# Splitting the first rotary query weights beside the retention stage's last gate tile, and the latents' first half in pieces of 256 columns

## The chip, the cores and the metric

The kernel runs on one core of a Trainium2 chip. A core has five engines with instruction queues of their own: PE (TensorE: matrix products, its weight loads shown as PEld), DVE (VectorE), ACT (ScalarE), POOL (GpSimd) and SP (SyncE, which here issues nearly all DMAs). Each works through its own queue in the order in which the program was built and waits there on semaphores. The metric is the device time of one execution in microseconds (us); lower is better.

## The reference, cut to what matters

One layer of a hybrid decoder: 1024 prompt tokens and 32 sample tokens, all in float32. Both pass through a retention branch and an attention branch over compressed latents; the branches are gated, merged and added to the input.

```python
# mixer_inputs: one projection of the normalised input gives all of these
z = rmsnorm(x, ln_w) @ w_in
rq, rk, rv, rg, cq, ckv, kr, mg, ga, gb = split(z)      # mg: attention's SiLU gate
q = (rmsnorm(cq, q_norm_w) @ w_uq).reshape(b, s, MLA_HEADS, MLA_QK)   # 8 heads of 128 + 64
q_nope, q_rope = q[..., :128], rope(q[..., 128:], pos)
ckv, kr = rmsnorm(ckv, kv_norm_w), rope(kr, pos)
# mla_prompt: latents (384 for queries, 256 for keys and values) of 1024 tokens
kv = (ckv @ w_ukv)                                       # k_nope, v per head
sc = (q_nope . k_nope + q_rope . kr) * scale             # causal softmax, then p @ v
# finish_layer
h_mla = (mla_o * silu(mg)) @ w_down_mla
```

## The kernel before

**Precision.** Each float32 operand is split in two parts: `hi`, a rounded copy made by ACT or POOL, and `lo`, the remainder, made by DVE (`lo_of`, line 199). A product is three matmuls (`mac`, lines 265, 266 and 267: hi by hi, the two mixed ones). In the profile's names a pair reads `wh`/`wl` (weights), `xh`/`xl` (normalised input), `lh`/`ll` (latents), `krA`/`krB` (rotary keys).

**Weights.** `stage` (lines 245, 246) loads a piece of weights into a staging tile `wr` with an SP DMA, makes `hi` and `lo`. There are two staging tiles, and two pairs of weight tiles `wh`, `wl`. Who makes `hi` is set by `hi_by[0]`: `act.copy` in the retention stage, `hi_pool` (POOL) from the start of prompt attention on.

**Stages around the change.** Retention runs head by head. Beside the last head's chunks and the sample tokens' state update (`sample_state`, lines 978 to 1057) stands a filler: the last three tiles of the gate `mg` (`gate_tiles`, tiles 5, 6 and 7). A tile has 8 x 128 weight rows against three thirds of 352 tokens, so 24 matmuls a third; ACT evacuates a third (`gev`, line 416) and SP stores it (line 417, `mg_95` is tile 5, `mg_96` tile 6, `mg_97` tile 7). The latents `lat` and rotary keys `krT` are loaded in the meantime from a scratch area in device memory to slots of the tags `qkA` and `qkB`.

Then the retention pools close, and prompt attention opens: its tiles take the memory of the retention stage, `krA` and the mask `above` that of the last head's output tiles `g`, the split latents `lh`, `ll` and the split rotary query weights `wqr` that of the normalised input. `rope_weights(0)` loads and splits three pieces (128 x 256) of `w_uq`; `split_latents` splits five latents of 1024 columns in halves of 512; `rope_queries` makes the first four heads' rotary query parts, eight tiles of 128 tokens with nine matmuls each, woven with head 0's queries, keys and values.

**What sets the order.** The code yields estimated costs and `woven` mixes streams by them, and then a scheduler sets the order in each engine's queue, so that an instruction may stand far from its place in the code. Only marked matmuls (`keep_in_program_order`, line 1041) are held.

Of the kernel before, what the change touches and what calls it, by code (L numbers as in the profile page):

```python
# [9 lines left out]
F32 = mybir.dt.float32  # L10
# [3 lines left out]
AF = mybir.ActivationFunctionType  # L14
# [5 lines left out]
P = 128  # L20
D = 1024
SEQ = 1024
# [11 lines left out]
HM = 8  # L34
NOPE = 128
ROPE = 64
# [7 lines left out]
C_RQ, C_RK, C_RV, C_RG, C_LAT, C_MG, C_GA, C_GB = 0, 1024, 2048, 4096, 6144, 6848, 7872, 8896  # L44
# [70 lines left out]
def woven(*streams):  # L115

    live = [[g, float(total), 0.0] for g, total in streams]
    while live:
        s = min(live, key=lambda e: e[2] / e[1])
        cost = next(s[0], None)  # L120
        if cost is None:
            live.remove(s)
            continue
        s[2] += cost
        yield cost
# [30 lines left out]
def run(g):  # L156
    for _ in g:
        pass
# [3 lines left out]
def decode_step(ctx: ExitStack, tc: tile.TileContext, A: dict, O: dict):  # L162
    nc = tc.nc
    pe, act, dve, pool, sp = nc.tensor, nc.scalar, nc.vector, nc.gpsimd, nc.sync

    const = ctx.enter_context(tc.tile_pool(name="const", bufs=1))
    wst = ctx.enter_context(tc.tile_pool(name="wst", bufs=2))
# [20 lines left out]
    def slots(pl, tag, bufs):  # L188

        return lambda name, shape=(P, NT), dt=F32R: pl.tile(list(shape), dt, tag=tag, name=name, bufs=bufs)  # L190

    def b32(ap):
        return ap.bitcast(F32)
# [4 lines left out]
    def lo_of(out, src, hi):  # L198
        dve.tensor_tensor(out=out, in0=src, in1=b32(hi), op=ALU.subtract)  # L199
# [4 lines left out]
    def C(name, i=0, w=None, rows=P):  # L204
        o, ww = at[name]
        w = ww if w is None else w
        return cst[:rows, o + i * w:o + (i + 1) * w]
# [10 lines left out]
    mgD = [dram.tile([P, NT], F32, tag=f"mg{f}", name=f"mg{f}") for f in range(8)]  # L218
# [7 lines left out]
    def small(pl, tag, w=1, bufs=4):  # L226
        return pl.tile([P, w], F32, tag=tag, name=tag, bufs=bufs)
# [9 lines left out]
    hi_by = [hi_pool]  # L237
# [11 lines left out]
    def wtiles():  # L249
        return tuple(wst.tile([P, 8, P], F32R, tag=t, name=t, bufs=2) for t in ("wh", "wl"))  # L250

    def load_w(src, nk):

        hi, lo = wtiles()
        src = src.rearrange("(k p) f -> p k f", p=P)
        for k in range(0, nk, 4):
            ks = slice(k, min(k + 4, nk))
            stage(src[:, ks], hi[:, ks], lo[:, ks])
        return hi, lo

    def mac(out, w, x, first, last):

        wh, wl = w
        xh, xl = x
        pe.matmul(out, wh, xh, start=first, stop=False)  # L265
        pe.matmul(out, wh, xl, start=False, stop=False)  # L266
        pe.matmul(out, wl, xh, start=False, stop=last)  # L267

    def gemm(w, xs, evac, nk, thirds_=range(3)):

        for j in thirds_:
            ps = mm()
            sl = slice(j * TH, (j + 1) * TH)
            for k in range(nk):
                mac(ps[:, :TH], (w[0][:, k, :], w[1][:, k, :]), (xs[k][0][:, sl], xs[k][1][:, sl]), k == 0, k == nk - 1)
                if k == nk - 1:
                    evac(j, ps[:, :TH], sl)
                yield 0.441
# [131 lines left out]
    def gate_tiles(col, dst, fs, func):  # L410
        for f in fs:
            w = load_w(w_in[:, col + f * P:col + (f + 1) * P], 8)

            def evac(j, ps, sl, f=f):
                t = wst.tile([P, TH], F32, tag="gev", name="gev", bufs=2)
                act.activation(t, ps, func)  # L416
                sp.dma_start(dst[f][:, sl], t)
            yield from gemm(w, xn, evac, 8)

    def chain(*gs):  # L420
        for g_ in gs:
            yield from g_
# [4 lines left out]
    def page_rows():  # L427
# [6 lines left out]
        row = small(p1, "row", NB * NPG // 16, 1)  # L434
        dve.tensor_reduce(out=row, in_=own, axis=AX.X, op=ALU.add)
        dve.tensor_scalar(idx, row, C("mod"), None, op0=ALU.add)
# [157 lines left out]
    def new_tokens(g):  # L594
# [20 lines left out]
        dve.tensor_tensor(out=pn, in0=sc[:H, :NR], in1=cst[:H, o:o + NR], op=ALU.add)  # L615
        dve.tensor_reduce(out=nm[:H], in_=pn, axis=AX.X, op=ALU.max, negate=True)
        act.activation(pn, pn, AF.Exp, bias=nm[:H], accum_out=l[:H])
# [150 lines left out]
    qkA, qkB = slots(qk8, "qkA", 4), slots(qk8, "qkB", 4)  # L768
# [16 lines left out]

    def head_qk(h, X):
        for name, col in (("q", C_RQ), ("k", C_RK)):
            dst = X[name] = [tok(f"{name}{m}", dt=F32) for m in range(2)]

# [23 lines left out]
            for m, evac in enumerate((first, second)):  # L813
                w = load_w(w_in[:, col + h * DK + m * P:col + h * DK + (m + 1) * P], 8)
                yield from gemm(w, xn, evac, 8)
            own = X[name + "S"] = p4.tile([P, 2, NR], F32, tag=name + "S", name=name + "S", bufs=2)
            for m in range(2):
                act.copy(own[:, m], dst[m][:, SEQ:])

    def head_w(h, X):  # L820

        parts = [[sl_("wv", (P, 2, DV)) for _ in range(4)] for sl_ in (qkA, qkB)]
        X["W"] = [tuple(part[k // 2][:, k % 2, :] for part in parts) for k in range(8)]
        for k in range(8):
            stage(w_in[k * P:(k + 1) * P, C_RV + h * DV:C_RV + (h + 1) * DV], *X["W"][k])
            yield 1.0
# [155 lines left out]
    def sample_state(h, X):  # L982
# [79 lines left out]
        else:  # L1062
            gate_out(h, on, NR, sl, g)
            yield 0.5

    def head_in(h, X):
        return woven((head_qk(h, X), 42.3), (head_w(h, X), 8.0))

    X = {}
    run(head_in(0, X))  # L1070
    for h in range(HR):
        chunks = prompt_chunks(h, X)
        for cost in chunks:
            if cost is None:
                break
        nxt = {}
        if h + 1 < HR:
            rest = (head_in(h + 1, nxt), 50.3)
        else:
            rest = (gate_tiles(C_MG, mgD, range(5, 8), AF.Silu), 31.8)  # L1080
            raws = [(qkB if i < 4 else qkA)("lat", (P, SEQ), F32) for i in range(5)]
            for i, raw in enumerate(raws):
                sp.dma_start(raw, latD[4 * i:4 * i + 4].rearrange("b i t -> (b i) t"))
            krT = qkA("krT", (P, SEQ), F32)
            for r in range(0, P, ROPE):
                sp.dma_start(krT[r:r + ROPE], latD[20:].rearrange("b i t -> (b i) t"))
        run(woven((chain(chunks, sample_state(h, X)), 27.9 if h + 1 < HR else 32.4), rest))
        X = nxt
    hi_by[0] = hi_pool
# [5 lines left out]
    ot = slots(mph.enter_context(tc.tile_pool(name="mla", bufs=1, side="right")), "ot", HM)  # L1095
# [19 lines left out]
        lo_of(lo, ps, hi)  # L1115

    lat = [tuple(latp.tile([P, SEQ], F32R, tag=f"l{s}{i}", name=f"l{s}{i}") for s in "hl") for i in range(5)]
    def split_latents(some):
        for u in range(2):
            us = slice(u * 512, (u + 1) * 512)  # L1120
            for i in some:
                hi, lo = (v[:, us] for v in lat[i])
                (hi_pool if i == 1 and u == 0 else act.copy)(hi, raws[i][:, us])
                lo_of(lo, raws[i][:, us], hi)
                yield 0.1

# [6 lines left out]
            split(krT[:, us], krA[:, us], krB[:, us])  # L1133
            yield 0.1

    HB = 4

    def rope_weights(h0):
        if h0:
            hi, lo = (v.rearrange("p (k x) d -> p k (x d)", k=4)[:, :3] for v in wtiles())  # L1140
        else:
            hi, lo = (ot("wqr", (P, 3, HB * ROPE)) for _ in range(2))
        for k in range(3):
            if k % 2 == 0:
                raws_ = wst.tile([P, 2, HB, ROPE], F32, tag="wr", name="wr", bufs=2)
            raw = raws_[:, k % 2]
            sp.dma_start(raw, A["w_uq"][0, k * P:(k + 1) * P, :].rearrange("p (h d) -> p h d", h=HM)[:, h0:h0 + HB, NOPE:])
            parts = [v[:, k].rearrange("p (h d) -> p h d", h=HB) for v in (hi, lo)]
            hi_by[0](parts[0], raw)
            lo_of(parts[1], raw, parts[0])  # L1150
        return hi, lo

    first_w = rope_weights(0)
    run(split_latents(range(3)))

    def rope_queries(h0, X):

        qrN = X["qrN"] = p5.tile([P, 8, HB * ROPE], F32, tag="qrN", name="qrN", bufs=1)
        hi, lo = rope_weights(h0) if h0 else first_w
        for t in range(8):  # L1160
            ps = mm() if h0 else ac()
            ts_ = slice(t * P, (t + 1) * P)
            for k in range(3):
                mac(ps[:, :256], (cqn[k][0][:, ts_], cqn[k][1][:, ts_]), (hi[:, k], lo[:, k]), k == 0, k == 2)
            rope_nat(qrN[:, t, :].rearrange("p (h d) -> p h d", h=HB), ps[:, :256].rearrange("p (h d) -> p h d", h=HB), t, P, p5, HB, "qro")
            yield 1.0
# [185 lines left out]
    for h in range(HM):  # L1352
        ahead = prep(h + 1) if h + 1 < HM else iter(())
        owed = 0.0
        if h + 1 == HM:
# [6 lines left out]
            first_w = load_w(A["w_down_mla"][0, :, :P], 8)  # L1362
# [128 lines left out]
    for f in range(8):  # L1491
# [3 lines left out]
        hi, lo = xr_("x1h"), xr_("x1l")  # L1495
# [10 lines left out]
        if f in (3, 4):  # L1506
            k = f - 3
# [73 lines left out]
    for j in range(3):  # L1581
        u = third(j, pT)
# [43 lines left out]
```

## Time and profile before

| | |
|---|---|
| median of 3 runs | 2147.01 us (2147.0 to 2148.47) |
| profiled execution | 2157.48 us, span 2155.6 us |
| mean granted TensorE clock | 0.996 |
| PE busy | 2112.4 us, 98% of the span |
| DVE, ACT, POOL busy | 58%, 34%, 15% |
| DMA | 307.84 MB, mean 143 GB/s |

The profile is of one execution, and its times are told from the span's start. The gate tiles' last part and the opening lie between about 1300 and 1380 us. A row of the timeline gives start, duration, engine, line and operation, result<-operands, count, and in brackets the idle time of the engine before it and what ended it. A row of a view by windows gives the stretch, its length, busy time (and instructions) of PE, PEld, DVE, ACT and POOL, then the granted clock (1.00 is full), the DMA engines' busy share and the transfer rate in GB/s. A row of waits gives who waited for whom, the total in us, how often and the longest.

### The profile page before, as it was taken

The numbers are of one execution on the slowest core, as the hardware profiler recorded it, in microseconds if no ns is written. First come the engines' busy times: TensorE is split into PE (matmuls) and PEld (weight loads), VectorE is DVE, ScalarE is ACT, GpSimd is POOL, SyncE is SP. The second block draws the span as 40 slices with busy tenths as digits, with TensorE's granted clock in tenths as the row PEclk, the third lists the DMA queues.
The fourth block names the chain that finished last, engine by engine and source line by source line (L and its number), as shares of the span: only waits on it lengthen the run. The fifth ranks groups of instructions, "written<-read, shape, count | busy, mean of one in ns | idle before, by whom it ended". The sixth has DMA issues, their size and how long they took to land. (4 is left out here: it accounts for less than half of the span.)

```text
span 2155.6 us, 38512 instructions
## 1 busy us (share of the span) xinstructions
PE 2112.4 (98%) x15192; PEld 1841.9 (85%) x15192; DVE 1260.7 (58%) x2846; ACT 724.1 (34%) x1528; POOL 326.7 (15%) x519
## 2 busy tenths in 40 slices
PE   8999999999999999999999999899999999999998
PEld 7898777777778897888888887788888999999998
DVE  5534555565655346667676774877777353444465
ACT  5412222433433222222222221454556341222243
POOL 2210111111100022222122220122221000000022
PEclk9999999999999999999999999999999999999999
DMA  7476656566565332553634628220112453324243
GB/s 209 123 223 225 238 185 231 200 245 222 186 239 176 112 85 65 162 158 103 217 72 126 198 74 265 69 53 12 38 57 81 143 178 100 95 84 126 79 143 118
DMA packets 325877, 307.84 MB, mean 143 GB/s; under 512 B 91648, under 2 KB 283264, under 8 KB 321600
## 3 DMA queue, kind: packets, MB, share of 16 engines
q1 hardware_dynamic: 316480, 221.50, 34.3%
q0 software_dynamic: 9216, 83.89, 10.3%
q8 instruction: 119, 1.95, 0.4%
q14 instruction: 62, 0.51, 0.1%
HBM read 236.96 MB, written 68.36 MB: 142 GB/s over the span
## 5 line engine op out<-in xcount | busy, mean ns | idle before, releaser
L265 PE MATMUL mm<-xh,wh 128*128 128x352 f32 x1344 | 456.6, 340 | 0.9 <-ACT gev L416 0.8
L267 PE MATMUL mm<-xh,wl 128*128 128x352 f32 x1344 | 435.2, 324 | 2.1 <-DVE wl L199 2.1
L266 PE MATMUL mm<-xl,wh 128*128 128x352 f32 x1344 | 436.1, 324 | 0.0
L265 PEld LDWEIGHTS mm<-xh,wh 128*128 128x128 f32 x1344 | 253.2, 188 | 91.5 <-issue 77.2
L266 PEld LDWEIGHTS mm<-xl,wh 128*128 128x128 f32 x1344 | 254.3, 189 | 3.2 <-issue 1.0
L267 PEld LDWEIGHTS mm<-xh,wl 128*128 128x128 f32 x1344 | 253.9, 189 | 3.3 <-DVE wl L199 2.6
L199 DVE TENSOR_TENSOR wl<-wr,wh 128x512 fp32r<-128x512 f32 (+2 forms) x251 | 172.9, 701 | 121.2 <-ACT wh L246 99.6
L246 ACT CAST wh<-wr 128x512 fp32r<-128x512 f32 x216 | 129.7, 618 | 291.9 <-PE mm L266 215.6
L651 DVE STREAM_TRANSPOSE kt<-craw 128x512 f32<-128x512 f32 x256 | 160.8, 681 | 108.3 <-PE sc L655 73.2
L416 ACT ACTIVATE gev<-mm 128x352 f32<-128x352 f32 x120 | 55.4, 463 | 231.6 <-PE mm L267 149.8
L265 PE MATMUL mm<-mh,wh 128*128 128x352 f32 x384 | 124.6, 325 | 1.4 <-ACT mh L1109 0.8
L266 PE MATMUL mm<-ml,wh 128*128 128x352 f32 x384 | 124.6, 325 | 0.8 <-DVE ml L199 0.6
L267 PE MATMUL mm<-gh,wl 128*128 128x352 f32 x384 | 124.3, 324 | 0.0
L267 PE MATMUL mm<-mh,wl 128*128 128x352 f32 x384 | 124.3, 324 | 0.0
L265 PE MATMUL mm<-gh,wh 128*128 128x352 f32 x384 | 124.2, 324 | 0.0
L266 PE MATMUL mm<-gl,wh 128*128 128x352 f32 x384 | 124.2, 323 | 0.0
L265 PE MATMUL mm<-wv,xh 128*128 128x512 f32 x256 | 103.7, 405 | 0.0
L266 PE MATMUL mm<-wv,xh 128*128 128x512 f32 x256 | 100.9, 394 | 0.0
L267 PE MATMUL mm<-wv,xl 128*128 128x512 f32 x256 | 100.8, 394 | 0.0
L655 PE MATMUL sc<-kt,q 32*32 32x512 f32 x2560 | 92.9, 600 | 0.0
L854 ACT ACTIVATE on<-ac,gb,gs 128x512 f32<-128x512 f32 (+1 forms) x36 | 28.0, 777 | 179.6 <-DVE gb L852 179.6
L1556 POOL TENSOR_TENSOR xr<-x1h,x1l 128x352 f32<-128x352 f32 x24 | 27.1, 1152 | 389.4 <-DVE pT L199 311.3
(383 smaller groups left out, 4537.6 us busy)
## 6 DMA issues: line engine op xcount, KB each, us to landing
wr<-in_w_in_dram SPq DMA_DIRECT2D x144, 256.0 KB, 2.8
st<-in_state_ret_dram SPq DMA_DIRECT2D x32, 512.0 KB, 4.5
out_ret_sample_dram<-st SPq DMA_DIRECT2D x32, 512.0 KB, 3.2
wr<-in_w_ple_gate_dram SPq DMA_DIRECT2D x48, 256.0 KB, 2.9
gt<-gev SPq DMA_DIRECT2D x48, 176.0 KB, 1.9
gl<-go SPq DMA_DIRECT2D x16, 528.0 KB, 5.2
gate<-ga SPq DMA_DIRECT2D x16, 528.0 KB, 3.6
g<-gt SPq DMA_DIRECT2D x32, 256.0 KB, 3.4
```

The lines of the kernel that those rows point to most:

```text
L199: dve.tensor_tensor(out=out, in0=src, in1=b32(hi), op=ALU.subtract)
L246: hi_by[0](hi, raw)
L265: pe.matmul(out, wh, xh, start=first, stop=False)
L266: pe.matmul(out, wh, xl, start=False, stop=False)
L267: pe.matmul(out, wl, xh, start=False, stop=last)
L416: act.activation(t, ps, func)
L651: dve.transpose(kt[:, 2 * i + s].rearrange("p (n r) -> p n r", r=32), src)
L655: pe.matmul(sc[32 * v:32 * v + 32, q, :], Q["q4"][qs_, j + v // 2, 2 * (g % 2) + v % 2, :], kt[qs_, v, :], start=n == 0, stop=n == NJ // 2 ...
L854: act.activation(on[:n], po, AF.Identity, bias=nb[:n], scale=s[:n])
L1556: pool.tensor_tensor(out=xr, in0=b32(x1[f][0][:, sl]), in1=b32(x1[f][1][:, sl]), op=ALU.add)
```

## The change

`rope_weights` moves ahead in the code and is called for the first four heads between gate tiles 6 and 7, as a part of the filler (`early`). Its `wqr` tiles take slots of the tag `qkB` instead of prompt attention's `ot`; to make room, three of the five latents move to `qkA` and two stay in `qkB`. At that point `hi_by[0]` is `act.copy`, so ACT makes the `hi` parts of `wqr`, not POOL. `split_latents` takes its pieces as an argument, and the three query latents' first half is split in two pieces of 256 columns; the second half stays whole.

```diff
+    def rope_weights(h0):
+        if h0:
+            hi, lo = (... for v in wtiles())
+        else:
+            hi, lo = (qkB("wqr", (P, 3, HB * ROPE)) for _ in range(2))
+        for k in range(3):
+            if k % 2 == 0:
+                raws_ = wst.tile([P, 2, HB, ROPE], F32, tag="wr", name="wr", bufs=2)
+            raw = raws_[:, k % 2]
+            sp.dma_start(raw, A["w_uq"]...[:, h0:h0 + HB, NOPE:])
...
+            hi_by[0](parts[0], raw)
+            lo_of(parts[1], raw, parts[0])
+        return hi, lo
...
-            rest = (gate_tiles(C_MG, mgD, range(5, 8), AF.Silu), 31.8)
-            raws = [(qkB if i < 4 else qkA)("lat", (P, SEQ), F32) for i in range(5)]
+            raws = [(qkA if i < 3 else qkB)("lat", (P, SEQ), F32) for i in range(5)]
...
+            def early():
+                first_w.extend(rope_weights(0))
+                yield 0.0
+            rest = (chain(gate_tiles(C_MG, mgD, range(5, 7), AF.Silu), early(), gate_tiles(C_MG, mgD, range(7, 8), AF.Silu)), 31.8)
...
-    def split_latents(some):
-        for u in range(2):
-            us = slice(u * 512, (u + 1) * 512)
+    def split_latents(some, parts=((0, 512), (512, SEQ))):
+        for a, b in parts:
+            us = slice(a, b)
             for i in some:
                 hi, lo = (v[:, us] for v in lat[i])
-                (hi_pool if i == 1 and u == 0 else act.copy)(hi, raws[i][:, us])
+                (hi_pool if i == 1 and a < 512 else act.copy)(hi, raws[i][:, us])
                 lo_of(lo, raws[i][:, us], hi)
...
-            hi, lo = (ot("wqr", (P, 3, HB * ROPE)) for _ in range(2))
...
-    first_w = rope_weights(0)
-    run(split_latents(range(3)))
+    run(split_latents(range(3), ((0, 256), (256, 512), (512, SEQ))))
```

The instructions' order as built shows where the scheduler puts the moved steps. SP's queue from the first store of gate tile 6 to tile 7's, before:

```order
L417 DMA mg_96<-gev 128x352
L978 DMA st<-in_state_ret_dram 128x2x512 x2
L1049 DMA out_ret_sample_dram<-st 128x2x512 x2
L417 DMA mg_96<-gev 128x352
L978 DMA st<-in_state_ret_dram 128x2x512 x2
L1049 DMA out_ret_sample_dram<-st 128x2x512 x2
L417 DMA mg_96<-gev 128x352
L1147 DMA wr<-in_w_uq_dram 128x4x64
L1049 DMA out_ret_sample_dram<-st 128x2x512 x2
L417 DMA mg_97<-gev 128x352
L1147 DMA wr<-in_w_uq_dram 128x4x64 x2
```

The same stretch of SP's queue with the change:

```order
L417 DMA mg_96<-gev 128x352
L978 DMA st<-in_state_ret_dram 128x2x512 x2
L1049 DMA out_ret_sample_dram<-st 128x2x512 x2
L417 DMA mg_96<-gev 128x352
L978 DMA st<-in_state_ret_dram 128x2x512 x2
L1049 DMA out_ret_sample_dram<-st 128x2x512 x2
L417 DMA mg_96<-gev 128x352
L245 DMA wr<-in_w_in_dram 128x4x128 x2
L245 DMA wr<-in_w_uq_dram 128x3x128
L245 DMA wr<-in_w_ukv_dram 128x2x128 x2
L1049 DMA out_ret_sample_dram<-st 128x2x512 x2
```

The two loads of tile 7's weights (`in_w_in_dram`) stand here now, behind tile 6's last store. Before, they stood where the last head's first key blocks (`kD`) are written, and the query weights' loads stand at that place now, as the difference of SP's queue there shows:

```order
-L245 DMA wr<-in_w_in_dram 128x4x128 x2
-L896 DMA knl<-kD_7994 128x256
+L1077 DMA wr<-in_w_uq_dram 128x4x64 x2
+L896 DMA knl<-kD_7994 128x256
+L1077 DMA wr<-in_w_uq_dram 128x4x64
```

ACT's queue from the sample values' copy (`vs`) to the sample state's (`xsb`), in the difference (`gev` are the gate thirds' evacuations):

```order
 L1009 COPY vs<-ac 64x512
-L246 CAST wh<-wr 128x512
-L416 ACTIVATE gev<-mm 128x352
-L246 CAST wh<-wr 128x512
-L416 ACTIVATE gev<-mm 128x352 x3
+L1079 CAST wqr<-wr 128x256 x3
+L416 ACTIVATE gev<-mm 128x352 x4
+L246 CAST wh<-wr 128x512 x2
 L1054 COPY xsb<-ac 128x512
```

Tile 7's casts `wh` stood ahead of the last four evacuations of tiles 5 and 6 and now stand behind them all; the three `wqr` casts are in their place. On PE, the sample state's four last L1045 matmuls now stand between tile 6's last matmul and tile 7's first (`xh_112`), where they followed six matmuls of tile 7 and the L1038 group. PE's queue there, with the change:

```order
L265 MATMUL mm<-xh_126,wh 128x352
L266 MATMUL mm<-xl_127,wh 128x352
L267 MATMUL mm<-xh_126,wl 128x352
L1045 MATMUL ac<-vst,kx 128x512 x2
L1045 MATMUL tr<-vst,kx 128x512 x2
L265 MATMUL mm<-xh_112,wh 128x352
L266 MATMUL mm<-xl_113,wh 128x352
```

At the opening, DVE does the remainders of the latents' pieces behind `krB`, in the place of `wqr`'s three, and the second latent's two pieces stand ahead of the first's; DVE's queue with the change:

```order
L199 TENSOR_TENSOR krB<-krT,krA 128x512
L199 TENSOR_TENSOR ll_14152<-lat,lh_14151 128x256 x2
L199 TENSOR_TENSOR ll_14150<-lat,lh_14149 128x256
L199 TENSOR_TENSOR ll_14154<-lat,lh_14153 128x256
L199 TENSOR_TENSOR ll_14150<-lat,lh_14149 128x256
```

`ll_14150`, `ll_14152` and `ll_14154` are the three query latents' remainders, whose first use on PE is in that order.

More of the change, by code (lines that the diff above doesn't have):

```diff
@@ L1064, in sample_state @@
             yield 0.5
+    HB = 4
+    def rope_weights(h0):
+        if h0:
+            hi, lo = (v.rearrange("p (k x) d -> p k (x d)", k=4)[:, :3] for v in wtiles())
+        else:
[4 more added lines that the diff above has]
+            raw = raws_[:, k % 2]
+            sp.dma_start(raw, A["w_uq"][0, k * P:(k + 1) * P, :].rearrange("p (h d) -> p h d", h=HM)[:, h0:h0 + HB, NOPE:])
+            parts = [v[:, k].rearrange("p (h d) -> p h d", h=HB) for v in (hi, lo)]
+            hi_by[0](parts[0], raw)
+            lo_of(parts[1], raw, parts[0])
+        return hi, lo
     def head_in(h, X):
         return woven((head_qk(h, X), 42.3), (head_w(h, X), 8.0))
-    X = {}
+    X, first_w = {}, []
     run(head_in(0, X))
@@ L1134, in rope_keys @@
             yield 0.1
[L1136 to L1141, printed above, removed]
-            hi, lo = (ot("wqr", (P, 3, HB * ROPE)) for _ in range(2))
[L1143 to L1151, printed above, removed]
-    first_w = rope_weights(0)
-    run(split_latents(range(3)))
+    run(split_latents(range(3), ((0, 256), (256, 512), (512, SEQ))))
     def rope_queries(h0, X):
```

## The prediction

> **What bounds the kernel now.** I read the page first, then TensorE's own waits, then the order of time around the two places that the change touches.
>
> ```profile
> span 2155.6 us, 38512 instructions
> PE 2112.4 (98%) x15192; PEld 1841.9 (85%) x15192; DVE 1260.7 (58%) x2846; ACT 724.1 (34%) x1528; POOL 326.7 (15%) x519
> ...
> wr<-in_w_in_dram SPq DMA_DIRECT2D x144, 256.0 KB, 2.8
> ```
>
> TensorE (PE) is busy for 98% of the span, so no work on another engine counts unless it makes PE wait, and a gain can only come out of PE's idle time. That idle time is listed by cause (total, times, longest, in us):
>
> ```profile
> PE ac L265 <- POOL wqr L196: 1.7, 1, 1.7
> PE ac L1038 <- DMA st<-in_state_ret_dram: 1.0, 1, 1.0
> PE ac L267 <- DVE ll L199: 0.9, 1, 0.9
> ```
>
> Two of these rows stand at the opening of prompt attention. In order of time (start, duration, instruction, idle before it and who ended it), on PE, then ACT, then POOL, then DVE:
>
> ```profile
> 1351.83 0.32 PE L267 MATMUL mm<-xh,wl 128*128 128x352 f32 x1
> 1353.85 0.35 PE L265 MATMUL ac<-wqr,lh 128*128 128x256 f32 x1 [1.70 <-POOL wqr L196]
> 1354.51 0.28 PE L266 MATMUL ac<-wqr,lh 128*128 128x256 f32 x1
> 1355.71 0.39 PE L267 MATMUL ac<-wqr,ll 128*128 128x256 f32 x1 [0.93 <-DVE ll L199]
> 1360.10 0.50 PE L267 MATMUL mm<-lh,wl 128*128 128x512 f32 x1 [0.54 <-DVE wl L199]
> ...
> 1351.74 1.14 ACT L1109 CAST krA<-krT 128x512 fp32r<-128x512 f32 x2 [2.92 <-DMA go<-g]
> 1352.79 0.46 ACT L416 ACTIVATE gev<-mm 128x352 f32<-128x352 f32 x1
> 1353.14 4.78 ACT L1123 CAST lh<-lat 128x512 fp32r<-128x512 f32 x9
> ...
> 1352.30 1.74 POOL L196 TENSOR_SCALAR wqr<-wr 128x256 fp32r<-128x256 f32 x3
> ...
> 1352.39 0.84 DVE L199 TENSOR_TENSOR krB<-krT,krA 128x512 fp32r<-128x512 f32 x1 [0.48 <-ACT krA L1109]
> 1353.16 1.90 DVE L199 TENSOR_TENSOR wqr<-wr,wqr 128x256 fp32r<-128x256 f32 x3
> 1354.98 4.20 DVE L199 TENSOR_TENSOR ll<-lat,lh 128x512 fp32r<-128x512 f32 x6
> 1366.34 0.41 DVE L199 TENSOR_TENSOR wl<-wr,wh 128x256 fp32r<-128x256 f32 x1
> ```
>
> The last gate matmul ends at 1352.15. PE then stands for 1.70, 0.93 and 0.54 us, 3.17 us in all. The first is put down to POOL, but ACT's first latent cast, 1353.14 plus about 0.57, ends as late; the second is DVE, which does 0.84 us of krB and 1.90 us of wqr before the first latent remainder.
>
> **The opening, as changed.** Three wqr casts leave POOL and three subtractions leave DVE here. ACT still does krA and the gate store first (to 1353.14). Its first cast then has 256 columns. Nine casts of 512 take 4.78 us, 0.53 each, so a half lies between 0.27 and 0.53; I take 0.36, since instructions have a fixed part. PE starts at 1353.14 + 0.36 + 0.13 = 1353.63 instead of 1353.85 (0.13 is what the start took before after the cast's end), so 1.48 us idle. DVE: krB ends at 1353.23, then come two pieces of the second latent (0.41 each by the last row, about 0.35 when they follow each other), then the first latent's, which ends near 1354.35. PE has four matmuls by then at 0.12 each (1353.85 to 1354.51 holds six starts), up to 1354.1: about 0.2 us idle. The query weights' remainder is ready long before (0.54 goes). What is late next is DVE's order, the second latent's pieces ahead of the first's. Idle 1.6 instead of 3.17: **−1.6 us**. Bounds: 0 (go's store keeps ACT as late, and pieces cost more than halves) and −3.17. The three more casts and subtractions lie on engines that are 34% and 58% busy and run beside PE; uncovered, a piece costs some 0.2 us.
>
> **The query weights' load and split.** Three 128 KB loads take the place of two weight loads on SP near 1223.94 (row below): one issue more, some 0.5 us, ahead of kD's stores. The list of PE's waits has nothing between 1200 and 1300, so 0; without that cover PE's next chunk would wait those 0.5 us. The casts stand on ACT behind vs, in 3.48 us of idle time (row below), three at about 0.36. DVE's three (1.90 us) stand ahead of the sample state's vr; the 1.78 us of idle time ahead of vr (1315.67) covers all but about 0.1 us, and PE uses vr's remainder later. Cost 0; uncovered, 0.1 us. The latents' other slots change only who waits for whose tile, of tiles long read: 0, and if a key evacuation did wait, under the 0.6 us of one cast.
>
> **The last gate tile's weights.** This is the costly part. The staging buffer has two slots, and the query weights now sit in them where the last gate tile's did. Rows of SP, ACT, DVE and PE, where L1045 at 1329.52 stands for the group as it comes around in each turn of the sample state:
>
> ```profile
> 1223.94 0.99 SPq L245 DMA_DIRECT2D wr<-in_w_in_dram  x2
> 1328.39 0.34 SPq L417 DMA_DIRECT2D mg<-gev  x1
> 1331.57 1.38 SPq L1049 DMA_DIRECT2D out_ret_sample_dram<-st  x2
> 1334.19 0.34 SPq L417 DMA_DIRECT2D mg<-gev  x1
> 1334.58 1.47 SPq L1147 DMA_DIRECT2D wr<-in_w_uq_dram  x1
> ...
> 1316.67 0.62 ACT L246 CAST wh<-wr 128x512 fp32r<-128x512 f32 x1 [3.48 <-PE mm L266]
> 1333.70 0.47 ACT L416 ACTIVATE gev<-mm 128x352 f32<-128x352 f32 x1 [5.34 <-PE mm L267]
> ...
> 1315.67 0.69 DVE L1019 CAST vr<-tr 128x512 fp32r<-128x512 f32 x1 [1.78 <-PE tr L1017]
> 1317.32 0.69 DVE L199 TENSOR_TENSOR wl<-wr,wh 128x512 fp32r<-128x512 f32 x1 [0.18 <-ACT wh L246]
> ...
> 1329.52 0.50 PE L1045 MATMUL ac<-vst,kx 32*128 32x512 f32 x2
> 1329.96 0.43 PE L265 MATMUL mm<-xh,wh 128*128 128x352 f32 x1
> 1333.30 0.32 PE L267 MATMUL mm<-xh,wl 128*128 128x352 f32 x1
> 1336.74 1.05 PE L1038 MATMUL ac<-st,qm 128*32 128x512 f32 x4 [1.05 <-DMA st<-in_state_ret_dram]
> ```
>
> Before, these weights are asked for at 1223.94 and wait 90 us in the slots; ACT casts them at 1316.67, when tile 5's matmuls free the weight buffer. In the new order SP issues them behind the store of tile 6's last third. That store goes out at 1334.19, after ACT's evacuation, so the load goes out where the first query-weight load did, at 1334.58. PE finishes tile 6 at 1333.62. Now ahead of tile 7 it has only the four L1045 matmuls (0.44 us, 1329.52 to 1329.96): PE runs dry at about 1334.05.
>
> When does the load land? Its own median is 2.8 us (page). But the queue is full: two 512 KB state stores left at 1331.57, and PE still waited at 1336.74 for a state load issued before them. Two views: the transfer rate in two stretches (last number, GB/s), and, of another stretch, the landing of one weight load issued at 1192.7 behind two 512 KB state loads (last number, us):
>
> ```profile
> 1334.50:1336.50 2.00, 1.14 (x5) 0.14 (x4) 0.00 (x0) 0.00 (x0) 0.00 (x0) 1.00 0.95 355
> 1334.50:1340.00 5.50, 4.40 (x24) 2.32 (x24) 1.75 (x3) 0.58 (x1) 0.00 (x0) 1.00 0.85 306
> ...
> wr<-in_w_in_dram SPq DMA_DIRECT2D x1, 256.0 KB, 6.0
> ```
>
> Before, 5.5 x 306 = 1.68 MB moved until the queue was empty, 0.13 MB of it the query weights that are gone from here. With the new 0.26 MB, 1.81 MB have to pass: 5.9 us at the mean rate, 5.1 at the 355 of the fuller first two us. I take 5.6 us from issue to landing, nearer to the 6.0 of the congested load than to 2.8, since more stands ahead here. The ends are 2.8 and 7. Landing 1340.2, ACT's cast 0.62, hand-over 0.1: PE resumes at 1340.9, **+6.9 us** idle. DVE's remainder (0.69) comes after the cast, and two matmuls cover part: **+0.4**. The second load lands about 0.7 us later, behind twelve matmuls: 0. SP's next loads wait for DVE to free each slot, and DVE now has a query-weight subtraction ahead of the last state update; the next user of that state's slots on PE (L1056) stands two matmul groups of 18 and 6 later: 0, up to 0.5 if DVE is late. The 1.05 us wait at 1336.74 goes, since that state has landed meanwhile: **−1.05**.
>
> **The clock.** A long idle stretch has a second price. Early in this trace PE waits 1.91 us, and the granted clock (the number after POOL's) falls:
>
> ```profile
> 27.66 0.40 PE L355 MATMUL tr<-cst,rs_r 32*128 32x32 f32 x2 [1.91 <-POOL rs_r L234]
> ...
> 29.00:29.50 0.50, 0.50 (x4) 0.50 (x3) 0.50 (x4) 0.50 (x4) 0.00 (x0) 0.75 0.84 131
> 29.50:32.50 3.00, 3.00 (x15) 2.96 (x14) 1.57 (x7) 2.65 (x8) 0.74 (x2) 0.50 0.62 108
> 32.50:33.00 0.50, 0.50 (x5) 0.50 (x5) 0.00 (x0) 0.50 (x2) 0.00 (x0) 0.84 0.78 138
> ...
> 1351.00:1356.00 5.00, 2.37 (x16) 1.90 (x15) 3.83 (x7) 4.26 (x9) 2.87 (x5) 1.00 0.52 167
> ```
>
> Lost there: 0.25 x 0.5 + 0.5 x 3 + 0.16 x 0.5 = 1.7 us. The opening's 1.70 and 0.93 cost no clock (last row), so such short waits may or may not. 6.9 us is over three times the longest of them: I take **+1.7**; bounds 0 and 3.4, two such stretches. [...]
>
> **Sum.** 6.9 + 0.4 − 1.05 + 1.7 − 1.6 = +6.35, about 6.4 us. The profiled execution took 2157.48 us (span 2155.6), the median of the timed runs is 2147.01, 10.5 less; the difference in us should carry over. 2157.5 becomes 2163.9, and **2147.0 becomes 2153.4**, +0.30%. What this measurement can tell from no change is 0.2%, 4.3 us.
>
> **The rivals.**
> - The clock stays at 1.00 through the wait: +4.7, 2151.7. For it, the waits at 1352; against it, the drop at 29. 0.15.
> - The load passes the backlog and lands in 2.8 us: PE resumes at 1338.1, 4.05 idle, so +1.8, with the clock +3.5: 2148.8 to 2150.5, within 0.2%. For it, the page's median; against it, the 6.0. 0.15.
> - Not slower: the weights are there when tile 6 ends, and only the opening counts: −1.6, 2145.4. It decides if the load is out by 1334.05 − 0.72 − 5.6 = 1327.7, ahead of the store of tile 6's second third at 1328.39. For it, the slots are free from about 1316; against it, SP works in order. 0.06. Even if both places lost every wait, 3.17 + 1.05 = 4.2 us would not be 0.2%.
> - The smaller pieces gain nothing at the opening, since go's store still holds ACT: +8.0, 2155.0. 0.04.
>
> **How the numbers follow.** My forecast, held load and half clock, has 0.60. Slower by over 0.2%: 0.60 + 0.04 + 0.09 of the steady clock's 0.15 = 0.73. Within: the other 0.06 + 0.15 + 0.03 of the early load = 0.24. Faster: the remaining 0.03. The range runs from the quick landing without clock loss, +2 (2149.0), to a landing of 7 us with 3.4 us of clock, 6.35 + 1.4 + 1.7 = +9.5, rounded up to +10 (2157.0).
>
> **What would show it.** Right: a PE wait of about 7 us before tile 7's first L265, ended by ACT's wh cast, itself ended by a DMA; a granted clock near 0.5 for some 3 us after it; no state wait at L1038; at the opening one wait near 1.5 and a short one on ll, none on wl. Wrong: a weight load issued before tile 6's second store, a landing under 4 us, or an idle time at the opening above 3.

## The result, and the profile after

The changed kernel takes 2155.38 us (median of 5 runs, 2149.86 to 2156.17), the kernel before 2147.0 (5 runs, 2144.41 to 2148.47): a ratio of 1.0033 (of the means), 95% interval 1.0021 to 1.0044, so +7.1 us (4.5 to 9.4); the two medians lie 8.4 apart. The forecast was +6.4, 2153.4.

The profiled executions stand the other way round (span 2155.6 before, 2148.1 with the change), so their spans can't be compared. First the head of the page of the changed kernel, then one stretch of both traces (200 to 720 us, where both run the same code in the same order; columns: length, busy us of PE, PEld, DVE, ACT, POOL, granted clock, DMA share, GB/s), before first:

```profile
span 2148.1 us, 38513 instructions
PE 2106.9 (98%) x15192; PEld 1841.2 (86%) x15192; DVE 1260.2 (59%) x2849; ACT 726.1 (34%) x1533; POOL 324.3 (15%) x517
```

```profile
200.00:720.00 520.00, 515.25 (x5680) 395.47 (x5679) 294.56 (x517) 170.38 (x277) 54.15 (x63) 1.00 0.59 206
```

```profile
200.00:720.00 520.00, 520.00 (x5769) 404.21 (x5758) 296.66 (x529) 174.78 (x283) 54.15 (x63) 1.00 0.59 207
```

The trace of before lost 4.75 us of PE time here, ahead of everything that the change touches, and was 10.5 us above its own median; its second profiled execution (below) is busy for all 520.00 and has a span of 2143.6. So I compare two stretches inside the traces. Stretch 1 runs from the start of ACT's last evacuation of gate tile 6 to the start of the last matmul of tile 7 (1333.70 to 1351.83 before). Stretch 2 runs from there to POOL's first scaling of probabilities, L1279 before and L1282 after (1385.99 before). Behind it the two traces keep their distance: 7.48 us there, 7.5 at the end.

Now stretch 1 of the changed kernel. SP, ACT, DVE and PE:

```profile
1320.10 0.34 SPq L417 DMA_DIRECT2D mg<-gev  x1
1320.49 1.92 SPq L245 DMA_DIRECT2D wr<-in_w_in_dram  x2
...
1319.61 0.46 ACT L416 ACTIVATE gev<-mm 128x352 f32<-128x352 f32 x1 [5.13 <-PE mm L267]
1326.20 1.37 ACT L246 CAST wh<-wr 128x512 fp32r<-128x512 f32 x2 [6.12 <-DMA wr<-in_w_in_dram]
...
1326.85 1.44 DVE L199 TENSOR_TENSOR wl<-wr,wh 128x512 fp32r<-128x512 f32 x2 [8.41 <-ACT wh L246]
...
1319.46 0.50 PE L1045 MATMUL ac<-vst,kx 32*128 32x512 f32 x2
1326.87 0.66 PE L265 MATMUL mm<-xh,wh 128*128 128x352 f32 x1 [6.91 <-ACT wh L246]
...
1329.07 1.93 PE L1038 MATMUL ac<-st,qm 128*32 128x512 f32 x8
```

SP sends tile 7's weights right behind tile 6's last store. The first of the two loads lands 5.7 us later, ACT casts it, and PE stands still for 6.91 us where before it had work. The state wait at L1038 is gone: all eight stand in one row.

The opening, PE and ACT:

```profile
1346.17 0.36 PE L265 MATMUL ac<-wqr,lh 128*128 128x256 f32 x1 [1.24 <-ACT lh L1144]
...
1347.43 0.38 PE L267 MATMUL ac<-wqr,ll 128*128 128x256 f32 x1 [0.56 <-DVE ll L199]
...
1358.82 0.35 PE L265 MATMUL ac<-wqr,lh 128*128 128x256 f32 x1 [0.56 <-DVE qro L378]
...
1344.27 1.14 ACT L1130 CAST krA<-krT 128x512 fp32r<-128x512 f32 x2 [2.67 <-DMA go<-g]
...
1345.67 4.45 ACT L1144 CAST lh<-lat 128x256 fp32r<-128x256 f32 x10
```

The waits of 1.70 and 0.93 us have become 1.24 and 0.56, and that of 0.54 on `wl` is gone (before's second execution has none there either); a new one of 0.56 us, on a step of the rotary queries (L378), has come in. Yet stretch 2 is only 0.25 us shorter. The next view shows the main reason. It is the changed kernel in steps of 3.41 us (the clock is the number after POOL's):

```profile
1320.74:1324.15 3.41, 0.00 (x0) 0.00 (x0) 0.00 (x0) 0.00 (x0) 0.00 (x0) 1.00 1.04 388
1324.15:1327.56 3.41, 0.69 (x2) 0.50 (x2) 0.69 (x1) 1.23 (x2) 0.00 (x0) 0.50 0.42 127
1327.56:1330.98 3.42, 3.42 (x14) 1.34 (x13) 0.98 (x2) 0.01 (x1) 0.51 (x1) 0.50 0.33 96
1330.98:1334.39 3.41, 3.41 (x25) 3.41 (x22) 2.66 (x5) 0.78 (x2) 0.00 (x0) 1.00 0.44 158
1344.63:1348.04 3.41, 1.61 (x11) 1.15 (x11) 2.81 (x7) 3.41 (x10) 1.75 (x4) 1.00 0.77 242
1348.04:1351.46 3.42, 3.42 (x12) 2.84 (x11) 3.42 (x9) 2.08 (x4) 0.00 (x0) 0.50 0.04 13
1351.46:1354.87 3.41, 3.41 (x22) 3.00 (x22) 2.54 (x8) 1.11 (x2) 0.00 (x0) 1.00 0.00 0
```

The clock is at half from 1324.15 to 1330.98, as forecast, and again from 1348.04 to 1351.46, which the prediction did not have. Matmuls of 512 columns start 0.43 us apart there instead of 0.23.

All profiled executions of the study, in us (the half clock counted while PE had work; the lower rows are the runs of the next section):

| execution | stretch 1 | stretch 2 | half clock in 1 | half clock at the opening |
|---|---|---|---|---|
| before | 18.13 | 34.16 | no | no |
| before, again | 17.06 | 34.64 | no | yes |
| change | 24.99 | 33.91 | 4.1 | yes |
| change, 2nd, 3rd, 4th | 24.67, 24.63, 25.24 | 34.03, 33.92, 33.88 | 3.2, 3.4, 4.6 | yes, yes, yes |
| weights behind tile 7, pieces | 18.13 | 31.43 | no | no |
| weights behind tile 7, halves | 18.14 | 31.44 | no | no |
| load on POOL's queue | 17.84 | 34.07 | no | yes |
| pieces only | 17.62 | 34.45 | no | no |
| move only | 24.57 | 31.72 | 3.3 | no |
| change, PE kept busy | 23.32 | 32.29 | no | no |

The mean of the change's four is 24.88 + 33.94 = 58.8, that of before's two 17.60 + 34.40 = 52.0. The difference of 6.8 agrees with the measured 7.1 and lies well inside its interval.

### The profile page after: what moved, and what is told of

The parts are those of the page before. It is cut to its first block, busy times and chain, and to the rows that moved or that the text cites. A ratio compares the mean times of both kernels' runs of the same rounds, so it can differ in the third digit from the quotient of the medians.

```text
span 2148.1 us, 38513 instructions
## 1 busy us (share of the span) xinstructions
PE 2106.9 (98%) x15192; PEld 1841.2 (86%) x15192; DVE 1260.2 (59%) x2849; ACT 726.1 (34%) x1533; POOL 324.3 (15%) x517
```

## The experiments

My theory: tile 7's weights are asked for too late, since SP reaches their load only behind tile 6's last store; PE waits 6.9 us and then works at half clock. At the opening the change gains, but a second half clock takes the gain back. Rivals: the two staging slots rather than the queue; the pieces; work added near the last tile. Ratios are against the kernel before, measured beside them on the same chip (median 2155.2 us beside the first four runs, 2146.0 beside the next two).

**The query weights behind tile 7.**

```diff
-            rest = (chain(gate_tiles(C_MG, mgD, range(5, 7), AF.Silu), early(), gate_tiles(C_MG, mgD, range(7, 8), AF.Silu)), 31.8)
+            rest = (chain(gate_tiles(C_MG, mgD, range(5, 8), AF.Silu), early()), 31.8)
```

> As the change, but the query weights are asked for behind gate tile 7 instead of between tiles 6 and 7; the pieces of 256 columns stay. Theory (tile 7's weights are asked for 7 us too late, because SP's queue reaches them behind tile 6's last store): they are asked for early again, the PE wait of 6.9 us ahead of tile 7 and its half clock are gone, and the state wait at L1038 (about 1 us idle) is back. From tile 6's last evacuation to tile 7's last matmul the trace takes 18.1 us again, as before, not 25.0. Opening as in the change or better by up to 1.7 us, if the second clock drop hung on the first. Time: before minus 0 to 3 us. Rival A (what costs is that query weights pass through the staging slots and the engines' queues anywhere near the last tile): the stretch stays above 21 us and the time 3 us or more above before. Rival B (what costs is the clock at the opening, from the pieces): the stretch is short and the opening is slower than before by 2 us or more.

Measured: 0.9985 (0.9976 to 0.9994) of before, about −3.2 us (−5.2 to −1.3): faster than before, and so than the change, and just past the 0 to −3 that I expected. PE's waits of this kernel from 1310 to 1362 (us in total, times, longest):

```profile
PE ac L1038 <- DMA st<-in_state_ret_dram: 1.1, 2, 0.9
PE ac L265 <- ACT lh L1144: 1.0, 1, 1.0
```

Stretch 1 is that of before's first execution to 0.01 us, the state wait is back, and stretch 2 is 2.7 us shorter than before's, 2.5 shorter than the change's, more than the 1.7 that I allowed for. Rivals A and B fall. So the same early query weights cost nothing when they come one tile later.

**Tile 7's loads on POOL's DMA queue.** In `stage` the load goes by `load_by[0]`:

```diff
-        sp.dma_start(raw, src)
+        load_by[0].dma_start(raw, src)
...
+            load_by[0] = pool if col == C_MG and f == 7 else sp
             w = load_w(w_in[:, col + f * P:col + (f + 1) * P], 8)
+            load_by[0] = sp
```

> As the change, but tile 7's two weight loads are issued on POOL's DMA queue instead of SP's; their slots, casts and order are the same. Theory (what delays the load is its place in SP's queue, behind tile 6's last store): the load leaves as soon as its slot is free, some 5 to 10 us ahead of tile 6's last evacuation, the PE wait of 6.9 us goes, and so does the clock drop after it; the state wait is gone too. From tile 6's last evacuation to tile 7's last matmul: 16 to 18 us; time before minus 1 to 3 us. Rival A (it is the two slots: the load can't leave before the query weights' casts and remainders are done, late as well): the wait stays at 4 us or more, time before plus 3 to 7. Rival B (the transfers of the two queues collide: the state loads and stores hold the rate): load leaves early but lands late, wait 1 to 4 us.

Measured: 1.0001 (0.9992 to 1.001). Lines stand up to 4 lower here; L1042 is L1038, L982 the state load. POOL, ACT, SP and PE:

```profile
1311.90 1.66 POOL L245 DMA_DIRECT2D wr<-in_w_in_dram  x2 [12.12 <-DMA lat<-latD]
...
1318.79 1.31 ACT L246 CAST wh<-wr 128x512 fp32r<-128x512 f32 x2 [4.41 <-DMA wr<-in_w_in_dram]
...
1321.31 1.59 SPq L982 DMA_DIRECT2D st<-in_state_ret_dram  x2
...
1327.58 1.05 PE L1042 MATMUL ac<-st,qm 128*32 128x512 f32 x4 [1.26 <-DMA st<-in_state_ret_dram]
```

The load leaves at 1311.90 and is cast at 1318.79, 13 us ahead of tile 7: wait and half clock are gone there, and a slot was free. So SP's order held the load back, not the slots (rival A falls), and the change's loss of 7 us is gone. But the time is that of before, and not 1 to 3 us below it. Tile 6's last third takes 7.80 us from evacuation to evacuation (1324.94 to 1332.74) instead of 5.52 (1325.48 to 1331.00 in the run above; 5.5 to 6.0 in every other trace): PE waits 1.26 us in the middle of L1038 for a state whose load left 6.3 us earlier. And the opening fell to half clock, so its gain went too. The DMA engines show what the 0.5 MB ran into (the same 6 us, the run above first; last two numbers DMA share and GB/s):

```profile
1314.00:1320.00 6.00, 6.00 (x41) 4.70 (x40) 4.50 (x7) 1.53 (x4) 0.00 (x0) 1.00 0.79 268
```

```profile
1314.00:1320.00 6.00, 6.00 (x43) 4.68 (x39) 3.22 (x6) 1.53 (x3) 0.00 (x0) 1.00 1.04 320
```

That the state load is late because of this crowding is read from the two rows, not tested. My expected −1 to −3 us missed it. Before, the same 0.5 MB crossed 90 us earlier, outside the crowd (DMA share 0.63, 150 GB/s in the 6 us from 1223.94).

**The pieces alone.** The kernel before with `split_latents` taking its pieces as an argument, as in the change, and

```diff
-    run(split_latents(range(3)))
+    run(split_latents(range(3), ((0, 256), (256, 512), (512, SEQ))))
```

> The kernel before with the latents' first half split in pieces of 256 columns, and nothing else: the query weights are asked for and cast where they were. Theory: the stretch to tile 7's last matmul is that of before (18.1 us), and the opening's first wait shrinks from 1.70 to about 1.2 us; if a chain of short waits of TensorE is what halved the clock at the opening of the change, it may appear here as well and eat the gain. Time: before minus 1.5 to plus 0.5, that is, no difference that this measurement can tell. Rival (the pieces are what costs, by more instructions on ACT, POOL and DVE): 3 us or more above before.

Measured: 1.0000 (0.9992 to 1.0009). PE's waits and the order of POOL and ACT at the opening:

```profile
1350.76 0.35 PE L265 MATMUL ac<-wqr,lh 128*128 128x256 f32 x1 [1.50 <-POOL wqr L196]
...
1352.56 0.38 PE L267 MATMUL ac<-wqr,ll 128*128 128x256 f32 x1 [0.72 <-DVE ll L199]
...
1356.41 0.50 PE L265 MATMUL mm<-lh,wh 128*128 128x512 f32 x1 [1.34 <-POOL wh L196]
...
1349.43 1.74 POOL L196 TENSOR_SCALAR wqr<-wr 128x256 fp32r<-128x256 f32 x3
...
1354.08 2.65 POOL L196 TENSOR_SCALAR wh<-wr 128x384 fp32r<-128x384 f32 x2 [1.84 <-DMA wr<-in_w_uq_dram]
...
1350.27 4.96 ACT L1123 CAST lh<-lat 128x256 fp32r<-128x256 f32 x11
```

The first wait is 1.50, not 1.2. The row puts it down to POOL's query-weight casts, but the last of them ends at 1351.17, when PE is already at work. By the times, what ends it is ACT's cast of the first latent piece, from 1350.27 to 1350.66: PE starts 0.10 us later, as it did behind that cast before (1353.75 and 1353.85). The piece takes 0.39 us instead of 0.61, and the wait is shorter by just these 0.2 us; ACT reaches the cast no earlier than before, about 1.0 us after the last gate matmul. The next weights' cast then comes late enough for a new wait of 1.34. On the whole the pieces neither gain nor cost here (stretch 2: 34.45, before 34.16 and 34.64).

**The move alone** is the change with the latents split in halves of 512 again.

> The change without the pieces of 256 columns: the query weights are asked for between gate tiles 6 and 7, and the latents are split in halves of 512 as before. Theory: the PE wait ahead of tile 7 is 6.9 us again, the clock at half for about 4 us after it, the stretch from tile 6's last evacuation to tile 7's last matmul 25 us. The opening's first wait is about 1.7 us again (ACT's lh of 512 columns), that on the query weights' remainder is gone. Time: before plus 6 to 8 us, no less than the whole change's 7.1 within 1.5. Rival (the pieces carry most of the loss): before plus 0 to 3 us.

Measured: 1.0022 (1.0013 to 1.0031), +4.7 us (2.8 to 6.7).

```profile
PE mm L265 <- ACT wh L246: 6.9, 1, 6.9
PE ac L265 <- ACT lh L1144: 1.5, 1, 1.5
PE ac L267 <- DVE ll L199: 0.4, 1, 0.4
```

The wait of 6.9 is there, and the opening, with halves of 512, is 2.4 us shorter than before. The move carries both the loss and the opening's gain. Its total is below the 6 to 8 us expected. In its one profiled execution no half clock followed the opening (a line of the clock's grid, explained below, fell between its two waits of 1.46 and 0.37), and the L378 wait of the change is absent; whether that holds in the timed runs isn't shown, and the interval reaches the change's.

**The query weights behind tile 7, with halves of 512**: the first run with `run(split_latents(range(3)))`.

> The query weights are asked for behind gate tile 7, as in the run before that was faster, but the latents are split in halves of 512 columns as before the change. Theory: the opening's gain comes from the query weights being ready ahead of it, not from the pieces. The stretch to tile 7's last matmul stays at 18.1 us; from there to the first L1279 of POOL about 31.7 us (34.16 before, 31.72 with the move alone, 31.43 with both); the first wait of TensorE is about 1.5 us on ACT's lh of 512 columns. Time: before minus 1.5 to minus 3 us. Rival (the pieces carry the gain): the second stretch takes 33 us or more, and the time is that of before within 1 us. On the clock: any half-clock stretch in this trace begins on a line of the grid of 3.41 us, behind a stretch between two lines in which TensorE idled 1.7 us or more.

Measured: 0.9987 (0.9978 to 0.9996), about −2.8 us. Stretch 2 is 31.44, with the pieces it was 31.43: so the opening's gain of 2.7 us comes from the query weights and not from the pieces. One half-clock stretch of this trace, at 728, does not follow idle time; it is told of below.

**PE kept busy through the waits.** The change, with work that feeds nothing:

```diff
+            if n == 3 and h + 1 == HR:
+                warm = tr()
+                for _ in range(36):
+                    pe.matmul(warm[:, :TH], xn[0][0][:, :P], xn[1][0][:, :TH], start=True, stop=True)
...
+            for _ in range(9 if h0 == 0 and t == 0 else 0):
+                pe.matmul(ps[:, :256], hi[:, 0, :P], hi[:, 0], start=True, stop=True)
```

> The change, with work added that feeds nothing: 36 matmuls of 352 columns (5.8 us at full clock) in TensorE's order between the last L1045 and tile 7, where the change waits 6.9 us for the weights, and 9 of 256 columns (1.05 us) ahead of the opening's first query matmul. Theory (the waits cost twice, by their length and by the half clock that follows them): the weights land when they did, tile 7 starts as late, about 1 us of the wait is left, but the granted clock stays at 1.00 in both places. Tile 6's last evacuation to tile 7's last matmul: 24.99 minus 2.05 = 22.9 us, 22.5 to 23.3; from there to the first L1279 33.91 minus 1.7 = 32.2 us, 31.7 to 32.7. Time: the change minus 2.5 to 4 us. Rival (the half clock is set by something else, or costs nothing on this path): 25 us and 34 us, time of the change or up to 1 us above it.

Measured: 1.0022 (1.0013 to 1.0031), +4.7 us (2.8 to 6.7), 2.4 less than the change by its own comparison with before, just short of the 2.5 to 4 expected. The two intervals overlap, so the times alone don't decide; the traces do, where stretches 1 and 2 make 55.6 us against 58.8. PE, and the clock around both places:

```profile
1323.67 6.06 PE L1049 MATMUL tr<-xh,xh 128*128 128x352 f32 x36
1330.81 0.43 PE L265 MATMUL mm<-xh,wh 128*128 128x352 f32 x1 [1.07 <-ACT wh L246]
```

```profile
1322.00:1330.00 8.00, 7.74 (x49) 6.98 (x47) 0.23 (x1) 0.47 (x1) 0.00 (x0) 1.00 0.94 317
1330.00:1334.00 4.00, 3.19 (x20) 2.02 (x21) 1.92 (x3) 1.65 (x3) 0.00 (x0) 1.00 0.30 87
1347.50:1351.00 3.50, 2.78 (x20) 2.31 (x19) 3.20 (x8) 3.50 (x10) 1.04 (x2) 1.00 0.66 221
```

The weights land no earlier: tile 7 starts 7.42 us after tile 6's evacuation (7.26 in the change). The clock stays at 1.00, and from that start to tile 7's last matmul it takes 15.90 us instead of 17.73 (1326.87 to 1344.60): the half clock cost 1.8 us there. Stretch 2 is 32.29 instead of 33.9, so it cost 1.6 at the opening. Both places cost twice, once by the wait and once by the half clock behind it, as the theory says.

**The change again.** The same kernel, to see whether the opening's half clock is chance.

> The change itself, a second profiled execution, to see whether the half clock at the opening belongs to the program or to where the program happens to lie on the clock's grid. Theory (the granted clock is decided on lines 3.41 us apart that run through the whole trace, at another phase in each execution, by TensorE's idle time between two lines): the half clock behind the wait of 6.9 us is there again, from a line, for 3.41 or 6.83 us, 1.75 to 5.1 us of it after TensorE resumes. At the opening the waits are 1.24 and 0.56 us again; a half clock of 3.41 us follows only if both lie between the same two lines, which at this spacing happens in about a third of all phases; the phase can be read from the trace's other drops. With it, tile 7's last matmul to the first L1279 takes about 33.9 us, without it about 32.0. Rival (the opening's half clock follows from the program's waits): it is there again, and the stretch is 33.9 us, whatever the phase.

By a line of the grid I mean an instant at which a trace's granted clock changes, or one a whole number of steps of 3.413 us from it (see the last section); the phase is where the lines lie. The half clock came again, 34.03 us. Its lines lay at 1327.34 and 1351.24, seven times 3.413 us apart, and both waits (1348.61 to 1349.85, 1350.55 to 1351.11) between the same two. That fits both theories; so three more:

> The kernel before, a second profiled execution, to see whether its opening too can lose clock. In the first its waits of 1.70 and 0.93 us cost none; a line of the clock's grid (3.41 us apart) lay at 1353.62, inside the first wait, and split the idle time in 1.47 and 1.16. Theory (idle time between two lines decides): a half clock of 3.41 us follows here if no line lies so that it splits the two waits, that is, if 1.7 us or more of idle falls between the same two lines, which happens in about half of all phases. With it, tile 7's last matmul to the first L1279 takes 34.2 plus up to 1.7 us, without it 34.2. Rival (the program alone decides): no half clock, 34.2 us.

> The change, a third profiled execution; the first two both had the half clock at the opening, with both waits between the same two lines of the grid. Theory (phase decides): if a line lies between the start of the first wait plus 0.1 us and the end of the second less 0.1, so that less than 1.6 us of idle is left on either side of it, no half clock follows and tile 7's last matmul to the first L1279 takes about 32.2 us; else it follows, and 33.9 to 34.0. A line inside has a chance of about 0.65. Rival (the program alone decides): half clock, 33.9 to 34.0, wherever the lines are.

> The change, a fourth profiled execution, with the expectations of the third: no half clock at the opening and about 32.2 us if a line of the grid splits the two waits, 33.9 to 34.0 if none does; by the rival 33.9 to 34.0 in any case.

The change lost its clock at the opening all four times, each time with both waits between two lines; a line lay 1.87, 1.39, 1.46 and 2.14 us behind the end of the first wait. My chance of a third for each would make four of four very rare. As far as these executions show, the phase is not drawn anew in each of them: its lines, counted from the first instruction, lie at 3.19, 2.97, 2.87 and 3.10 us modulo 3.4133 for the change, and at 1.94 and 1.46 for the kernel before. The kernel before decides between the two theories. Its rows in steps of the grid, two of the first execution and two of the second:

```profile
1350.21:1353.62 3.41, 1.94 (x12) 1.64 (x11) 1.45 (x3) 1.88 (x4) 1.71 (x4) 1.00 0.46 114
1353.62:1357.03 3.41, 2.25 (x17) 2.08 (x18) 3.41 (x7) 3.41 (x8) 1.38 (x3) 1.00 0.70 233
```

```profile
1339.53:1342.94 3.41, 0.94 (x6) 0.77 (x6) 3.18 (x5) 3.41 (x8) 2.63 (x5) 0.99 0.70 217
1342.94:1346.35 3.41, 3.26 (x15) 3.26 (x16) 3.41 (x6) 2.35 (x5) 1.84 (x2) 0.51 0.47 134
```

The waits of the second, which answer to the 1.70 and 0.93 of the first:

```profile
1341.22 0.36 PE L265 MATMUL ac<-wqr,lh 128*128 128x256 f32 x1 [1.69 <-POOL wqr L196]
...
1343.09 0.58 PE L267 MATMUL ac<-wqr,ll 128*128 128x256 f32 x1 [0.94 <-DVE ll L199]
```

In the first a line at 1353.62, 181 steps behind the drop at 735.81, splits them (PE idle 1.47 and 1.16), and the clock holds; in the second they fall between two lines (2.47 idle), and the next 3.41 us run at half. The rival, that the program alone decides, falls with this. It costs the kernel before only 0.5 us (34.64 against 34.16).

## Why the prediction was right, point by point

- **The load.** Forecast: out behind tile 6's last store, landing after 5.6 us, PE idle 6.9. Measured: 5.7 and 6.91 (6.85 to 6.96 in four executions). This was the prediction's main step, and the rivals of an early or quick load fall.
- **The query weights' own load and split.** Forecast 0. Between 1200 us and tile 6's end the change's trace has no wait of PE. Right.
- **The clock at tile 7.** Forecast +1.7, bounds 0 to 3.4. Measured 1.8 (15.90 against 17.73), and 1.5 to 2.1 in the other three executions, where tile 7 took 17.36 to 17.97 us. Right.
- **DVE's remainder.** Forecast +0.4; no wait for it shows in the rows of the change, where half-speed matmuls cover the 1.44 us of both remainders: 0.
- **The state wait.** Forecast −1.05. It is gone, but it was no fixed term: the second execution of before has stretch 1 shorter by 1.07, with its eight L1038 in one row. So it is a term that varies: with tile 7's load in its old place stretch 1 takes 17.06 to 18.14 us in five traces. Against the mean of 17.60 stretch 1 costs +7.3, against 18.13 it costs +6.86; the forecast terms make +7.95.
- **The opening.** Forecast −1.6 from shorter waits. This step failed. The two waits did shrink (to 1.24 and 0.56, where 1.5 and a short one were forecast), though the one on L378, 0.56 us in all four executions, was not foreseen; its cause stays open. But stretch 2 fell by only 0.25, or 0.5 against both means. With the clock held at 1.00 (PE kept busy) it fell by 1.9 and more, so the opening would have gained about what was forecast, and the half clock took 1.6 back. The prediction took the clock of before's opening, 1.00, as given; there it hung on a line between two waits. And it gave the pieces a share: they shorten the first wait by 0.2 us, but the stretch not at all (31.43 against 31.44), while the query weights, ready ahead, are worth 2.7.

So the sum came out at +6.4 for a measured +7.1 with some luck, because two errors partly cancel: stretch 1 was set about 0.7 to 1.1 too high, the opening 1.1 to 1.4 too favourable. The rival in which the opening gains nothing from the pieces (+8.0) was near in this, and ACT does still wait for go's store (2.67 us ahead of `krA`); yet the opening's gain was there, and what took it was the clock.

## What to carry to other kernels

Here a transfer that was moved ahead through a staging buffer of two slots was paid for by the one that it displaced. So look for the load that had been waiting, long landed, in the slot, and put the newcomer behind the last such load (here one gate tile later: −3 us instead of +7). Price a wait of TensorE with the half clock that may follow it, and not by its length alone: here two short waits close together (1.24 and 0.56 us), both between two lines of the grid, were followed by a half clock that cost another 1.6. And a stall seen in one profiled execution is a term with a chance, not a fixed one, where a second execution may not show it.

## What the runs showed of the hardware

**The granted clock changed on a grid.** Every half-clock stretch that ends inside a trace's span lasts 3.41 or 6.83 us, and the lines lie a whole number of steps apart: in the changed kernel 78.28, 1324.15 and 1348.04 are 365.0 and 7.0 times 3.413 us apart (1269.76 us in 372 steps, 3.4133 us each). 1.80 us of idle in 3.41 were followed by a half clock (changed kernel, 1344.63) and 1.47 were not (before, 1350.21). The 1.6 and 1.7 us of the expectations lie between these two and are estimates; no run shows either as a threshold. Idle time alone doesn't draw the edge everywhere: early in the traces 1.55 us were followed by a half clock (weights behind tile 7 with pieces, 25.06) and 1.83 were not (before, 73.62).

**A half clock without idle time ahead of it.** At 728 the run with halves behind tile 7 falls to half clock behind a step in which PE counts as busy throughout:

```profile
725.05:728.46 3.41, 3.41 (x34) 3.41 (x32) 0.69 (x1) 1.44 (x3) 0.00 (x0) 1.00 0.14 53
728.46:731.87 3.41, 3.41 (x14) 3.41 (x14) 1.02 (x2) 0.00 (x0) 3.02 (x16) 0.50 0.43 101
```

That step is filled by matmuls of 32 columns (L744, 32 of them in 3.67 us, from 724.96). The group runs in every trace of the study. Where 3.00 us of it (before), 3.41 and 3.11 (the change, second and third), 3.37 (PE kept busy) and 3.41 (here) lay between two lines, a half clock followed; in the other seven traces, with at most 2.78, none did. These matmuls start 0.115 us apart, about as far as those of 256 columns at the opening (0.12); why a half clock follows them isn't shown.

In before's first execution this half clock lasted from 735.81 to 742.63. At half clock that is some 3.4 us lost, which with the 4.75 us of lost PE time makes most of the 10.5 us above its median. The change lost clock at this place in two of four executions. This stands ahead of everything that the change touches and outside both stretches, so it's part of the spread of the times and not of the 6.8 us.
